# Weight sums by accumulating loads, and more blocks of seven products in the feed-forward part

## The chip, the cores and the metric

One NeuronCore of a Trainium2 chip runs the whole program. The time is device microseconds of that core. The kernel before takes 1552.08 us (median of three runs, 1551.42 to 1552.7).

## The reference

One layer of a conditioned hybrid decoder on 256 rows of width 2048, all in float32. The change concerns the second half:

```python
h2 = modulate(rms_norm(x, norm2_g[l]), sh2, sc2)
gate, up = jnp.split(h2 @ w_ffn_in[l], 2, axis=-1)          # 2048 -> 2 x 5632
x = x + g2 * ((jax.nn.silu(gate) * up) @ w_ffn_out[l])      # 5632 -> 2048
return rms_norm(x, final_g)
```

Ahead of it stand the modulation (a matrix-vector product with a 2048 x 12288 weight), one projection to 11264 columns, a gated linear recurrence, banded attention and three projections back.

## The kernel before, in words

**Three products for one.** Every float32 operand is split into a high part `hi` (rounded to float32r) and a low part `lo` = value - `hi`. `mm3` computes hi·hi, hi·lo and lo·hi: three matmuls for one product. Weights come in pieces of 128 x 1024 float32 (512 KB, an *item*): a load by SP's queue into one of five `raw` buffers, `hi` by a cast on ScalarE (ACT, four buffers), `lo` by a subtraction on VectorE (DVE, three buffers), and then the products on TensorE (PE).

**The planner.** `step(i)` writes out the order of everything around item i: the load of item i+5, `made` (an item that is computed, not loaded) of item i+4, `hi` of item i+3, `lo` of item i+2, the stages hung ahead of the item (`before`), and its products. Work between two slabs (`posts`) and side work (`sides`) goes in between, by a table of costs. Each engine runs its own instructions in this order. The only waits are for data and for a buffer to come free.

**Seven products rather than eight.** A pair of k tiles (2 x 128 rows of a weight) with two blocks of 512 columns and two blocks of 128 rows of activations is a 2 x 2 by 2 x 2 product of blocks. `seven()` computes it with seven block products by Winograd's scheme, with sums of weight blocks and of activation blocks formed ahead. It makes four items: a and b, the two loaded weight pieces (three of the four blocks are used as they are), x, a tile of two sums of weight blocks (`first`, L418 and L419), and y, a tile of two more sums that build on x (`second`, L424 and L425). All four sums are VectorE instructions of 128 x 512, into tiles called `made` in the slabs and a region of `last` in the sweeps. A plain pair is 24 matmuls of 128x512, a seven 21.

**The feed-forward part.** Slab 0 uses a plain form. Slabs 1 to 10 (`add_pair`) each compute 512 gate and 512 up columns with eight pairs of k tiles. The pairs k = 4, 8, 12 go by seven products (`SEVEN_1`). Then the second weight is swept: the first sweep (n = 0) does columns 0 to 1023 over all 44 k tiles, the second (n = 2) columns 1024 to 2047 over the first 36, and a tail does the rest. In each sweep the pairs k = 6, 10, ..., 34 go by seven (`SEVEN`), with one plain pair between two sevens. `parts_high` and `parts_low` split the sums of activations for a seven of a sweep (the tiles `ah` and `al`, L1370 on VectorE).

**Buffers.** `b4` is a pool of 25 general tiles of 4 KB per partition. The activations h and h2 and, at the end, `last` (the residual rows x2, the final gain fg and two sum tiles) lie in a pool of their own (`hp`), the modulation's weights, `made` and `ah` in two more (`araw`). `Halves.fetch` (L467) loads the modulation's weights on SP's queue; an instruction on VectorE (L496) uses one up and so hands the buffer back.

Of the kernel before, what the change touches and what calls it, by code (L numbers as in the profile page):

```python
# [74 lines left out]
def hybrid_layer(  # L75
# [8 lines left out]
    hp = ctx.enter_context(tc.tile_pool(name="hp", bufs=1))  # L84
    bp = ctx.enter_context(tc.tile_pool(name="bp", bufs=N_B4))
# [310 lines left out]

    SUMS = 4

    def seven(loads, where, act, bank, begin, end, made_in, post=None):

        got = {}

# [12 lines left out]
        def first(i):
            got.update({0: live[i - 2][0], 1: live[i - 1][0]})
            x = got["x"] = made_in(0)
            nc.vector.tensor_tensor(x[:, 0:512], block(0, 1), block(0, 0), op=ALU.subtract)  # L418
            nc.vector.tensor_tensor(x[:, 512:], block(0, 1), block(1, 1), op=ALU.subtract)  # L419
            return x  # L420

        def second(i):
            y, x = made_in(1), got["x"]
            nc.vector.tensor_tensor(y[:, 0:512], block(1, 1), x[:, 0:512], op=ALU.subtract)  # L424
            nc.vector.tensor_tensor(y[:, 512:], block(1, 0), y[:, 0:512], op=ALU.subtract)  # L425
# [1276 lines left out]
```

## Time and profile before

| | |
|---|---|
| median of three runs | 1552.08 us |
| the profiled execution | 1549.47 us, its span 1547.7 us, granted clock 0.997 |
| loads of the first feed-forward weight in a slab pair's form | 176 of 512 KB, median 4.2 us to landing |
| loads in the first sweep, second sweep | 44 and 36 of 512 KB, 4.3 and 3.4 us |
| HBM read | 394.72 MB, 258 GB/s with the writes over the span |
| POOL | 11 instructions, 3.7 us |

In the profile PE, DVE, ACT, POOL and SP are the five engines, PEld the weight load of TensorE, L12 a line of the kernel, and "raw", "hi", "lo" tiles by name without their numbers. The shortest way through it goes from the chain that ended last to the stage in which the change lies, and from there to the engine with least slack in that stage.

### The profile page before, as it was taken

To read this page: it belongs to the slowest core of one execution; us is meant where nothing else is said; L and a number is where in the kernel's file an instruction comes from. 1 tells how busy PE (TensorE), PEld (TensorE's weight loads), DVE (VectorE), ACT (ScalarE), POOL (GpSimd) and SP (SyncE) were. 2 spreads that over 40 slices of the span, in tenths; PEclk is the share of its full clock that TensorE was granted. 3 is DMA by queue.
4 is the path that set the end of the run, shared out by engine and by line. 5 is a ranking of instruction groups with operands and counts; after the bars stand their busy time and mean duration, and the time that the engine had idled before them with its cause. 6 is when DMAs were issued, how large, how long until landed. Compare 5 with 4: busy or idle time off the path is not lost.

```text
span 1547.7 us, 22116 instructions
## 1 busy us (share of the span) xinstructions
PE 1530.9 (99%) x8013; PEld 1314.2 (85%) x8013; DVE 1392.2 (90%) x1854; ACT 858.2 (55%) x1113; POOL 3.7 (0%) x11
## 2 busy tenths in 40 slices
PE   8999999999999999999999999999999999999997
PEld 7999999998878887888888788888888888888786
DVE  7889989889888887988988899999999999998998
ACT  4654443776855445444545655555555556664664
POOL 0000000000000000000000000000000000000000
PEclk9999999999999999999999999999999999999999
DMA  9999998666887797999999665565555666766563
GB/s 367 343 320 345 341 315 291 212 203 208 270 275 264 259 328 274 368 339 339 366 384 346 191 202 187 194 198 200 200 192 200 207 193 236 251 206 204 189 212 128
DMA packets 112909, 400.37 MB, mean 259 GB/s; under 512 B 12432, under 2 KB 12576, under 8 KB 112416
## 3 DMA queue, kind: packets, MB, share of 16 engines
q1 hardware_dynamic: 112192, 397.39, 74.5%
q8 instruction: 62, 1.02, 0.3%
q0 software_dynamic: 320, 1.06, 0.2%
q10 hardware_dynamic: 288, 0.52, 0.1%
q14 instruction: 47, 0.39, 0.1%
HBM read 394.72 MB, written 4.20 MB: 258 GB/s over the span
## 4 chain that ended last, share of the span: by engine, by line
PE 93%; DMA 4%; DVE 2%; issue 1%; ACT 0%; SPq 0%; DVEq 0%; ACTq 0%
PE pf L1352 9%; PE f L356 7%; PE f L357 7%; PE f L355 7%; PE wi L357 6%; PE wi L355 6%; PE wi L356 6%; PE wga L357 2%; PE wga L355 2%; PE wga L356 2%; PE wa L357 2%; PE wa L355 2%; PE wa L356 2%; PE wl L356 2%; PE wl L357 2%; PE wl L355 2%
## 5 line engine op out<-in xcount | busy, mean ns | idle before, releaser
L305 ACT CAST hi<-raw 128x1024 fp32r<-128x1024 f32 (+1 forms) x540 | 536.9, 1002 | 447.3 <-PE wi L356 77.2
L317 DVE TENSOR_TENSOR lo<-raw,hi 128x1024 fp32r<-128x1024 f32 (+1 forms) x540 | 618.7, 1159 | 66.0 <-issue 35.0
L357 PE MATMUL wi<-h_both,lo 128*128 128x256 f32 x800 | 227.3, 284 | 3.6 <-DVE lo L317 3.6
L355 PE MATMUL wi<-h_both,hi 128*128 128x256 f32 x800 | 228.0, 285 | 0.0
L356 PE MATMUL wi<-h_both,hi 128*128 128x256 f32 x800 | 227.0, 284 | 0.0
L355 PE MATMUL f<-hi,h_both 128*128 128x512 f32 x460 | 180.2, 392 | 0.0
L357 PE MATMUL f<-hi,h_both 128*128 128x512 f32 x460 | 179.0, 389 | 0.0
L356 PE MATMUL f<-lo,h_both 128*128 128x512 f32 x460 | 179.0, 389 | 0.0
L357 PEld LDWEIGHTS wi<-h_both,lo 128*128 128x128 f32 x800 | 154.2, 193 | 4.0 <-DVE lo L317 4.0
L356 PEld LDWEIGHTS wi<-h_both,hi 128*128 128x128 f32 x800 | 154.3, 193 | 0.2
L355 PEld LDWEIGHTS wi<-h_both,hi 128*128 128x128 f32 x800 | 154.3, 193 | 0.2
L305 ACT CAST hi<-made 128x1024 fp32r<-128x1024 f32 x60 | 63.4, 1057 | 112.8 <-PE f L357 111.3
L496 DVE CUSTOM_DVE_ANT_0 aw<-aw,crow,vec 128x1024 f32<-128x1024 f32 x79 | 100.6, 1278 | 6.2 <-DMA aw<-in_ada_t_dram 6.2
L496 DVE CUSTOM_DVE_ANT_0 aw<-aw,crow,modc 128x1024 f32<-128x1024 f32 x79 | 100.9, 1280 | 3.0 <-DMA aw<-in_ada_t_dram 2.8
L357 PEld LDWEIGHTS f<-hi,h_both 128*128 128x128 f32 x460 | 86.3, 188 | 18.0
L355 PEld LDWEIGHTS f<-hi,h_both 128*128 128x128 f32 x460 | 86.4, 188 | 17.8 <-issue 0.2
L356 PEld LDWEIGHTS f<-lo,h_both 128*128 128x128 f32 x460 | 86.4, 188 | 17.8 <-issue 0.2
L317 DVE TENSOR_TENSOR lo<-made,hi 128x1024 fp32r<-128x1024 f32 x60 | 73.4, 1225 | 25.9 <-PE f L356 20.7
L1352 PE MATMUL pf<-hi,fc 128*128 128x512 f32 x256 | 71.0, 389 | 0.0
L305 ACT CAST hi<-last 128x1024 fp32r<-128x1024 f32 x32 | 33.7, 1054 | 52.5 <-PE pf L1352 49.2
L1352 PEld LDWEIGHTS pf<-hi,fc 128*128 128x128 f32 x256 | 48.1, 188 | 10.0
L355 PE MATMUL wl<-hi,yh 128*128 128x512 f32 x128 | 52.5, 410 | 0.0
(355 smaller groups left out, 2940.4 us busy)
## 6 DMA issues: line engine op xcount, KB each, us to landing
raw<-in_w_f_dram SPq DMA_DIRECT2D x176, 512.0 KB, 4.2
raw<-in_w_in_dram SPq DMA_DIRECT2D x164, 512.0 KB, 7.1
aw<-in_ada_t_dram SPq DMA_DIRECT2D x158, 512.0 KB, 6.5
raw<-in_w_f2a_dram SPq DMA_DIRECT2D x44, 512.0 KB, 4.3
raw<-in_w_f2d_dram SPq DMA_DIRECT2D x36, 512.0 KB, 3.4
raw<-in_w_lru_dram SPq DMA_DIRECT2D x32, 512.0 KB, 6.5
raw<-in_w_att_dram SPq DMA_DIRECT2D x32, 512.0 KB, 7.8
raw<-in_w_o_dram SPq DMA_DIRECT2D x32, 512.0 KB, 8.3
```

The lines of the kernel that those rows point to most:

```text
L305: nc.scalar.copy(hi[:, cs], live[i][0][:, cs])
L317: nc.vector.tensor_tensor(lo[:, cs], raw[:, cs], f32(hi[:, cs]), op=ALU.subtract)
L355: nc.tensor.matmul(ps, lhsT=lh, rhs=rh, start=start, stop=False, skip_group_check=True)
L356: nc.tensor.matmul(ps, lhsT=lh, rhs=rl, start=False, stop=False, skip_group_check=True)
L357: nc.tensor.matmul(ps, lhsT=ll, rhs=rh, start=False, stop=stop, skip_group_check=True)
L496: nc.vector.tensor_tensor_reduce(out=r, in0=r, in1=crow[:, j * CH:(j + 1) * CH], op0=ALU.mult, op1=ALU.add, scale=1.0, scalar=dst if j els ...
L1352: nc.tensor.matmul(bank(t, n), lhsT=l[:, rows(t)], rhs=w[:, c0:c0 + 512], start=kt == 0 and k == 0, stop=kt == (EARLY - 2 if (t, n) == (1, ...
```

## The change

- **Sums of x by transfers.** `first` computes nothing any more. `fill` issues, on POOL's queue, two loads of 128 x 512 from the weight in HBM into a tile `wx` 16 steps ahead, and `add`, 11 steps ahead, two more such loads that add into it (`accum_op`). `second` still does two VectorE sums. Signs of the sums on the activations' side and of the combinations after it change to match.
- **Loads of used columns only.** The raw loads of a seven fetch 1.5 of 2 halves.
- **More sevens.** Slabs 1 to 8: k = 4, 6, 10, 12 (four of eight pairs), slab 9: 4, 6, 10, slab 10: 4, 6. In a slab the pairs run plain, plain, seven, seven, plain, seven, seven, plain. Sweeps: ten of 18 pairs, with turns `--77-77-77-77-77--` (7 a seven, - a plain pair) where it was plain, plain and then seven and plain in turn.
- **One pool.** h, h2, the modulation's weights, `ah`, `wx`, the y tiles, x2 and fg all come from `b4`, now 35 tiles. x2 and fg are fetched in halves, at chosen items.
- `f_parts` handles slabs with no, one or two pairs by seven.

```diff
-SEVEN = tuple(range(6, 36, 4))
-
-SEVEN_1, SLAB_7 = (4, 8, 12), 1
+N_SUM = (16, 11)
+SEVEN = (6, 10, 12, 14, 18, 22, 24, 26, 30, 34)
+
+SEVEN_1, SLAB_7, LAST_7 = (4, 6, 10, 12), 1, (3, 2)
+
+TURNS = "--77-77-77-77-77--"
...
-    hp = ctx.enter_context(tc.tile_pool(name="hp", bufs=1))
-    bp = ctx.enter_context(tc.tile_pool(name="bp", bufs=N_B4))
+    bp = ctx.enter_context(tc.tile_pool(name="bp", bufs=N_B4 + N_H + N_ADA))
...
+    def do_sum(j):
+        def do(i):
+            if items[i].sums is not None:
+                items[i].sums[j]()
+                load_time(CH)
+        return do
...
-        nc.sync.dma_start(raw[:, :cols], src)
-        live[i] = [raw, None, None, load_time(cols)]
+        cs = items[i].used
+        nc.sync.dma_start(raw[:, cs], src)
+        live[i] = [raw, None, None, load_time(cs.stop - cs.start)]
...
+        upto("fill", do_sum(0), i + N_SUM[0])
+        upto("add", do_sum(1), i + N_SUM[1])
...
+        def fill():
+            x = got["x"] = bp.tile([P, CH], F32, tag="b4", name="wx")
+            for j in range(2):
+                nc.gpsimd.dma_start(x[:, j * 512:(j + 1) * 512], block(0, 1))
+
+        def add():
+            for j in range(2):
+                nc.gpsimd.dma_start(got["x"][:, j * 512:(j + 1) * 512], block(j, j), accum_op=ALU.add)
 
         def first(i):
-            got.update({0: live[i - 2][0], 1: live[i - 1][0]})
-            x = got["x"] = made_in(0)
-            nc.vector.tensor_tensor(x[:, 0:512], block(0, 1), block(0, 0), op=ALU.subtract)
-            nc.vector.tensor_tensor(x[:, 512:], block(0, 1), block(1, 1), op=ALU.subtract)
-            return x
+            return got["x"], 0
 
         def second(i):
-            y, x = made_in(1), got["x"]
-            nc.vector.tensor_tensor(y[:, 0:512], block(1, 1), x[:, 0:512], op=ALU.subtract)
-            nc.vector.tensor_tensor(y[:, 512:], block(1, 0), y[:, 0:512], op=ALU.subtract)
-            return y
+            def raw(*kn):
+                l, c0 = where[kn]
+                return live[i - 3 + l][0][:, c0:c0 + 512]
+
+            y = bp.tile([P, CH], F32, tag="b4", name="wy")
+            nc.vector.tensor_tensor(y[:, 0:512], got["x"][:, 0:512], raw(1, 1), op=ALU.add)
+            nc.vector.tensor_tensor(y[:, 512:], y[:, 0:512], raw(1, 0), op=ALU.add)
+            return y, 1.3
...
         def parts_high():
-            hi = parts[0] = wp.tile([P, 8, P], F32R, tag="araw", name=f"ah{n}_{k}", bufs=N_ADA)
+            hi = parts[0] = b4(f"ah{n}_{k}", F32R, (8, P))
...
-                    t = wp.tile([P, CH], F32, tag="araw", name=f"aw{self.n}", bufs=N_ADA)
+                    t = bp.tile([P, CH], F32, tag="b4", name=f"aw{self.n}")
...
-        others = [k for k in range(0, EARLY, 2) if k not in SEVEN]
-        turns = others[:2] + [k for two in zip(SEVEN, others[2:]) for k in two]
+        start = len(items)
+        kinds = {"7": iter(SEVEN), "-": iter(k for k in range(0, EARLY, 2) if k not in SEVEN)}
+        turns = [next(kinds[c]) for c in TURNS]
```

How the change moves instructions, at three places. In the rows a number after a name tells tiles apart.

VectorE in the first sweep, before: the seven of k = 14 (items 528 to 531: a, b, x, y) behind the plain item 527. Two more plain items follow.

```order
L317 TENSOR_TENSOR lo527_12416<-raw527_12381,hi527_12404 128x1024
L418 TENSOR_TENSOR last_12197<-raw528_12390 128x512
L419 TENSOR_TENSOR last_12197<-raw528_12390,raw529_12402 128x512
L317 TENSOR_TENSOR lo528_12430<-raw528_12390,hi528_12414 128x512
L1370 TENSOR_TENSOR al0_14_12432<-fs3_9722,ah0_14_12418 128x896
L424 TENSOR_TENSOR last_12197<-raw529_12402,last_12197 128x512
L425 TENSOR_TENSOR last_12197<-raw529_12402,last_12197 128x512
L317 TENSOR_TENSOR lo529_12452<-raw529_12402,hi529_12428 128x1024
L317 TENSOR_TENSOR lo530_12470<-last_12197,hi530_12450 128x1024
L317 TENSOR_TENSOR lo531_12479<-last_12197,hi531_12468 128x1024
```

The same place in the changed order, the second seven of a double (k = 14, items 544 to 547) right behind the first (k = 12, items 540 to 543):

```order
L454 TENSOR_TENSOR wy_12607<-wy_12607,raw541_12558 128x512
L337 TENSOR_TENSOR lo541_12612<-raw541_12558,hi541_12587 128x1024
L337 TENSOR_TENSOR lo542_12630<-wx_12408,hi542_12610 128x1024
L337 TENSOR_TENSOR lo543_12637<-wy_12607,hi543_12628 128x1024
L337 TENSOR_TENSOR lo544_12652<-raw544_12605,hi544_12635 128x512
L1418 TENSOR_TENSOR al0_14_12656<-fs31_9812,ah0_14_12642 128x896
L453 TENSOR_TENSOR wy_12666<-wx_12494,raw545_12626 128x512
L454 TENSOR_TENSOR wy_12666<-wy_12666,raw545_12626 128x512
L337 TENSOR_TENSOR lo545_12671<-raw545_12626,hi545_12650 128x1024
L337 TENSOR_TENSOR lo546_12683<-wx_12494,hi546_12669 128x1024
L337 TENSOR_TENSOR lo547_12692<-wy_12666,hi547_12681 128x1024
```

The two sums of x are gone. `lo` of b, x and y of one seven is now followed by a, `al` and the sums of y of the next, where a plain pair's two `lo` stood.

VectorE in the second slab pair, before: the seven of k = 12 (items 324 to 327) behind two computed and two plain items.

```order
L317 TENSOR_TENSOR lo320_9030<-made_8976,hi320_9005 128x1024
L317 TENSOR_TENSOR lo321_9043<-made_9002,hi321_9028 128x1024
L317 TENSOR_TENSOR lo322_9052<-raw322_9000,hi322_9041 128x1024
L317 TENSOR_TENSOR lo323_9064<-raw323_9026,hi323_9050 128x1024
L418 TENSOR_TENSOR made_9073<-raw325_9048,raw324_9039 128x512
L419 TENSOR_TENSOR made_9073<-raw325_9048 128x512
L317 TENSOR_TENSOR lo324_9078<-raw324_9039,hi324_9062 128x1024
L424 TENSOR_TENSOR made_9094<-raw325_9048,made_9073 128x512
L425 TENSOR_TENSOR made_9094<-raw324_9039,made_9094 128x512
L317 TENSOR_TENSOR lo325_9099<-raw325_9048,hi325_9076 128x512
```

In the changed order, the end of the first seven of a double (k = 4, x and y are items 322 and 323) and the second (k = 6, items 324 to 327):

```order
L337 TENSOR_TENSOR lo322_9080<-wx_8845,hi322_9055 128x1024
L337 TENSOR_TENSOR lo323_9091<-wy_9052,hi323_9078 128x1024
L337 TENSOR_TENSOR lo324_9101<-raw324_9050,hi324_9089 128x1024
L453 TENSOR_TENSOR wy_9115<-wx_8894,raw325_9076 128x512
L454 TENSOR_TENSOR wy_9115<-wy_9115,raw324_9050 128x512
L337 TENSOR_TENSOR lo325_9120<-raw325_9076,hi325_9099 128x512
L337 TENSOR_TENSOR lo326_9133<-wx_8894,hi326_9118 128x1024
L337 TENSOR_TENSOR lo327_9145<-wy_9115,hi327_9131 128x1024
```

Here too the sums into the x tile are gone, and the second seven's sums of y and `lo` follow the first seven's without a plain pair between.

POOL in the slab pairs. Before, POOL has no instruction there. Now each double has four fills (L438) and behind them four adds (L442), x2 standing for two alike:

```order
L438 DMA wx_8845<-in_w_f1_dram 128x512 x2
L438 DMA wx_8894<-in_w_f1_dram 128x512 x2
L442 DMA wx_8845<-in_w_f1_dram 128x512 x2
L442 DMA wx_8894<-in_w_f1_dram 128x512 x2
L438 DMA wx_9002<-in_w_f1_dram 128x512 x2
L438 DMA wx_9093<-in_w_f1_dram 128x512 x2
L442 DMA wx_9002<-in_w_f1_dram 128x512 x2
L442 DMA wx_9093<-in_w_f1_dram 128x512 x2
L438 DMA wx_9227<-in_w_f1_dram 128x512 x2
```

A fill or an add of the next double stands behind the adds of this one on POOL.

More of the change, by code (lines that the diff above doesn't have):

```diff
@@ L276, in __init__ @@
             self.used, self.before = slice(*(used or (0, cols))), list(before)
+            self.sums = None
     items = []
     live = {}
-    at = {"load": 0, "made": 0, "hi": 0, "lo": 0}
+    at = {"fill": 0, "add": 0, "load": 0, "made": 0, "hi": 0, "lo": 0}
+    def do_sum(j):
[4 more added lines that the diff above has]
+        return do
     def do_load(i):
@@ L397, in hybrid_layer, with seven @@
     SUMS = 4
-    def seven(loads, where, act, bank, begin, end, made_in, post=None):
+    def seven(loads, block, by_k, act, bank, begin, end, post=None):
         got = {}
+        where = {(k, n): (k, n * 512) if by_k else (n, k * 512) for k in range(2) for n in range(2)}
         def products(*jobs):
@@ L430, in seven @@
             jobs = [(a, where[kn][1], to) for a, kn, to in plain if where[kn][0] == l]
-            cs = [c0 for _, c0, _ in jobs]
+            cs = [where[kn][1] for _, kn, _ in plain if where[kn][0] == l]
+            used = (min(cs), max(cs) + 512)
             items.append(Item(
-                loads[l], CH, products(*jobs), weight=0.25 * len(jobs), used=(min(cs), max(cs) + 512),
+                loads[l][:, slice(*used)], CH, products(*jobs), weight=0.25 * len(jobs), used=used,
             ))
         items.append(Item(first, CH, products((3, 0, "r"), (5, 512, "u")), weight=0.5))
+        items[-1].sums = fill, add
         items.append(Item(second, CH, products((4, 0, "q"), (2, 512, "10")), post, weight=0.5))
@@ L1192, in h2act @@
     def h2act(kt):
-        return h2["both"][:, kt, 0, :], h2["both"][:, kt, 1, :]
+        return h2["parts"][kt]
     def gate_f_post(s):
@@ L1215, in f_parts @@
     def f_parts(s, pts):
-        if 4 * s + 2 not in SEVEN:
+        seven_ = [j for j in range(2) if 4 * s + 2 * j in SEVEN]
+        if not seven_:
             fh, fl = b4(f"fh{s}", F32R), b4(f"fl{s}", F32R)
@@ L1288, in add_pair @@
         start = len(items)
-        for k in range(0, NK, 2):
+        sevens = SEVEN_1[:LAST_7[s - 9]] if s > 8 else SEVEN_1
+        others = [k for k in range(0, NK, 2) if k not in sevens]
+        for k in others[:2] + list(sevens[:2]) + others[2:3] + list(sevens[2:]) + others[3:]:
             loads = [w_f1[s + 11 * n][:, k * 512:(k + 2) * 512] for n in range(2)]
-            if k in SEVEN_1:
-                last = k == SEVEN_1[-1]
+            if k in sevens:
+                last = k == sevens[-1]
                 seven(
-                    loads, {(0, 0): (0, 0), (1, 0): (0, 512), (0, 1): (1, 0), (1, 1): (1, 512)}, act(k), bank,
-                    k == SEVEN_1[0], last,
-                    lambda i: wp.tile([P, CH], F32, tag="araw", name="made", bufs=N_ADA), shared if last else None,
+                    loads, lambda j, n, k=k: w_f1[s + 11 * n][:, (k + j) * 512:(k + j + 1) * 512], False, act(k), bank,
+                    k == sevens[0], last, shared if last else None,
                 )
@@ L1299, in add_pair @@
             for n in range(2):
-                items.append(Item(loads[n], CH, plain(k, n), gated_rows if (k, n) == (NK - 2, 1) else None))
+                items.append(Item(loads[n], CH, plain(k, n), gated_rows if (k, n) == (others[-1], 1) else None))
         if s == SLAB_7:
@@ L1466, in hybrid_layer @@
                 ))
+        end = len(items)
+        if n == 0:
+            items[end - 12].before.append(fetch(0, 0, 1))
+        else:
+            items[start + 8].before.append(fetch(0, "fg"))
+            items[end - 14].before.append(fetch(1, 0, 1))
+            items[end - 6].before.append(fetch(1, "fg"))
     for i, k in enumerate(range(EARLY, NH, 2)):
```

132 lines of the change are left out of this document (73 added, 59 removed).

## Prediction

> **What bounds the kernel now.** I read the page's totals and its chain of waits first, then the busy time by stretch, then single instructions of one period.
>
> ```profile
> span 1547.7 us, 22116 instructions
> PE 1530.9 (99%) x8013; PEld 1314.2 (85%) x8013; DVE 1392.2 (90%) x1854; ACT 858.2 (55%) x1113; POOL 3.7 (0%) x11
> PE 93%; DMA 4%; DVE 2%; issue 1%; ACT 0%; SPq 0%; DVEq 0%; ACTq 0%
> ```
>
> TensorE sets the time, and VectorE has a tenth of the span left. The windows view shows the stages: the nine slab pairs between two equal instructions (927.20 to 1309.20), the first and the second sweep, and three stretches ahead of them.
>
> ```profile
> core 0: us, PE busy (x) PEld busy (x) DVE busy (x) ACT busy (x) POOL busy (x), PEclk, DMA share, GB/s
> 927.20:1309.20 382.00, 382.00 (x1724) 317.10 (x1723) 354.43 (x432) 216.65 (x252) 0.00 (x0) 1.00 0.60 198
> 1309.20:1400.00 90.80, 90.80 (x406) 75.29 (x405) 88.49 (x100) 58.25 (x65) 0.00 (x0) 1.00 0.68 238
> 1400.00:1500.00 100.00, 99.54 (x437) 81.49 (x436) 92.66 (x106) 58.02 (x67) 0.00 (x0) 1.00 0.60 200
> 100.00:200.00 100.00, 100.00 (x798) 98.34 (x797) 93.06 (x132) 43.97 (x51) 0.00 (x0) 1.00 0.94 338
> 700.00:800.00 100.00, 100.00 (x455) 82.98 (x454) 89.32 (x94) 46.79 (x66) 1.70 (x3) 1.00 1.00 360
> ```
>
> In the stages that change, TensorE is never idle, at a granted clock of 1.00; VectorE is busy 93% in the slab pairs and 97% in the first sweep. The DMA engines move 198 to 238 GB/s there, and TensorE stood at full busy elsewhere with 338 and 360. So removed matmuls shorten the time as long as VectorE keeps up, and VectorE is nearly full.
>
> What a late VectorE does shows in the chain at the start of the second sweep, and in the rows of the two engines there:
>
> ```profile
> 1445.91 1.23 DVE lo L317
> 1449.97 5.44 PE pf L1352 x24
> 1460.70 5.44 PE pf L1352 x24
> 1470.99 5.44 PE pf L1352 x24
> 1481.19 5.44 PE pf L1352 x24
> ...
> 1446.58 0.39 PE L355 MATMUL pr<-hi,ah 128*128 128x512 f32 x1
> 1447.19 0.50 PE L356 MATMUL pr<-lo,ah 128*128 128x512 f32 x1 [0.22 <-DVE lo L317]
> ```
>
> One 128x512 matmul takes 5.44/24 = 0.2267 us. A period of one plain pair (24 matmuls) and one block of seven products (21) is 45 x 0.2267 = 10.20 us, which the last two starts show; the two before are 10.73 and 10.29, so 0.53 + 0.09 us were stalls. The first matmul of an item needs only `hi`, the second needs `lo`: it came 0.61 us after the first, 0.06 us after its `lo` ended (1445.91 + 1.22 = 1447.13).
>
> **The change part by part.** *Products.* Sevens go from 10 x 3 + 2 x 8 = 46 to 8 x 4 + 3 + 2 + 2 x 10 = 57. Each saves one product, three matmuls: 33 x 0.2267 = **-7.5 us** (21 matmuls in the slabs, 4.8 us; 12 in the sweeps, 2.7 us). That stands only if TensorE stays fed.
>
> *VectorE in the sweeps.* One period of before, from its timeline (start, duration):
>
> ```profile
> 1340.41 0.39 PE L355 MATMUL pp<-hi,ah 128*128 128x512 f32 x1
> 1340.66 1.05 ACT L305 CAST hi<-last 128x1024 fp32r<-128x1024 f32 x1 [1.66 <-PE pf L1352]
> 1341.74 1.22 DVE L317 TENSOR_TENSOR lo<-last,hi 128x1024 fp32r<-128x1024 f32 x1 [0.29 <-ACT hi L305]
> 1342.88 2.35 DVE L317 TENSOR_TENSOR lo<-raw,hi 128x1024 fp32r<-128x1024 f32 x2
> 1345.15 0.69 DVE L418 TENSOR_TENSOR last<-raw 128x512 f32<-128x512 f32 x1
> 1345.76 0.68 DVE L419 TENSOR_TENSOR last<-raw,raw 128x512 f32<-128x512 f32 x1
> 1346.36 0.69 DVE L317 TENSOR_TENSOR lo<-raw,hi 128x512 fp32r<-128x512 f32 x1
> 1346.96 1.08 DVE L1370 TENSOR_TENSOR al<-fs,ah 128x896 fp32r<-128x896 f32 x1
> 1347.96 0.69 DVE L424 TENSOR_TENSOR last<-raw,last 128x512 f32<-128x512 f32 x1
> 1348.68 0.69 DVE L425 TENSOR_TENSOR last<-raw,last 128x512 f32<-128x512 f32 x1
> 1349.29 1.22 DVE L317 TENSOR_TENSOR lo<-raw,hi 128x1024 fp32r<-128x1024 f32 x1
> 1350.43 1.22 DVE L317 TENSOR_TENSOR lo<-last,hi 128x1024 fp32r<-128x1024 f32 x1
> ```
>
> Successive starts cost 1.14 us for a `lo` of 1024 columns, 0.60 for one of 512 or a sum, 1.00 for `al`, 1.33 for the two sums of y. The change takes the two sums of x (L418, L419) off VectorE: a seven costs 0.60 + 3 x 1.14 + 1.33 + 1.00 = 6.35 us there and was 7.55. But the new turns put two sevens side by side with one plain pair: 2 x 6.35 + 2 x 1.14 = 14.98 us of VectorE against (21 + 21 + 24) x 0.2267 = 14.96 of TensorE. There is no slack left, so the order within the period decides.
>
> Call the four items of the first seven a, b, x, y and those of the second a', b', x', y'; let TensorE begin a at 0. ACT's `hi` of y begins at 0.25, when a buffer comes free (1340.66 against 1340.41), and `lo` of y begins at 1.33 (1341.74). VectorE then has, in the order it is given, `lo` a' (+1.14), `al'` (+0.60), the two sums of y' (+1.00), `lo` b' (+1.33), which ends 1.22 later: 1.33 + 1.14 + 0.60 + 1.00 + 1.33 + 1.22 = 6.62. TensorE has finished the first seven at 21 x 0.2267 = 4.76, a' at 5.44, and wants `lo` b' at 5.67. With the 0.06 us of above it waits 6.68 - 5.67 = **1.0 us**. What follows is in time: `lo` x' ends at 6.62 + 1.14 = 7.76, wanted at 6.68 + 5 x 0.2267 + 0.2267 = 8.04. Before, a plain pair stood in this place, 5.44 us of TensorE for 2.28 of VectorE. Ten double sevens in the two sweeps: **+10 us**. The lower bound is the engine's own excess with the 0.29 us that it idles for `hi` once a period, 14.98 + 0.29 - 14.96 = 0.3 us, or +3; I take the upper, since the order is fixed.
>
> The work in the sweeps that is not periodic (the sums after the first sweep, the product with the final gain, L1451) cost about 0.6 us at the start of the second sweep, by the periods above. With no slack, the gain's 128x1024 product among the sums of y' comes on top, at most another 1.22 us; I take **+0.9**.
>
> *VectorE in the slabs.* The same chain, without `al` and with whole columns the other way round:
>
> ```profile
> 1108.15 0.39 PE L355 MATMUL fp<-hi,h_both 128*128 128x512 f32 x1
> 1108.39 1.06 ACT L305 CAST hi<-made 128x1024 fp32r<-128x1024 f32 x1 [1.66 <-PE f L357]
> 1108.19 2.58 DVE L317 TENSOR_TENSOR lo<-made,hi 128x1024 fp32r<-128x1024 f32 x2 [0.30 <-PE f L356]
> 1110.84 2.36 DVE L317 TENSOR_TENSOR lo<-raw,hi 128x1024 fp32r<-128x1024 f32 x2
> ```
>
> `lo` a' begins 2.69 us after a's start (1110.84), the sums of y' 1.14 later, `lo` b' after 1.33 and `lo` x' 0.60 after that, ending 2.69 + 1.14 + 1.33 + 0.60 + 1.22 + 0.06 = 7.04. Here a has two products and b one, so TensorE wants the second matmul of x' at 30 x 0.2267 + 0.2267 = 7.03. It just fits: **0 us**, but 0.1 us more in each of the 18 double sevens would cost 2.
>
> *The transfers.* Fills and adds need no slot of the raw ring, and each add is issued 11 steps ahead. Per seven they bring 2 x 0.524 MB, and the raw loads lose 0.262, so a slab pair goes from 16 x 0.524 = 8.39 MB (in 42.4 us: 198 GB/s, as the window shows) to 8.39 + 4 x 0.786 = 11.53 MB in 41.8 us, 276 GB/s; the second sweep goes from 18.9 to 26.7 MB in 91 us, 293 GB/s. Both lie under 338. That holds if an accumulating byte costs a plain one. No row shows an accumulating transfer. The nearest software transfers are these:
>
> ```profile
> L1021 POOL DMA_DIRECT2D g<-g1d x2 | 1.1, 541 | 5.3 <-DMA g1d<-g_row 5.3
> ...
> g<-g1d POOLq DMA_DIRECT2D x2, 512.0 KB, 8.6
> ...
> raw<-in_w_f_dram SPq DMA_DIRECT2D x176, 512.0 KB, 4.2
> ```
>
> An issue takes POOL 0.54 us: four per seven are 2.2 us on an idle engine. New waits: an add waits on POOL for its fill, with only later fills behind it; ACT's `hi` of x waits for the add, with every later `hi` behind it, and so TensorE. From the add's place to that `hi` are seven steps of 41.8/24 = 1.74 us, 12.2 us, against 8.6 us to landing in the row. Below, an accumulate that costs nothing still moves nothing earlier: 0. Above, at three plain bytes each, the second sweep would be 26.7 + 2 x 5.24 = 37.2 MB, 103 us at 360 GB/s instead of 91, and the DMA engines would set the pace. I take **0**, near the plain rows, and keep the other end as a rival.
>
> The Trainium skill speaks against that: Collectives: The Full Stack, in the section on the bandwidth ceiling, says that a transfer that adds is slow not for the addition but for its two reads, which both go on the same ring. Two reads per added byte would make 31.9 MB in the second sweep, an estimate of 351 GB/s, just inside the 360 of the window above; by it the sum stays as it is, with nothing to spare. No run here shows it yet.
>
> *Waits that go.* The buffers of the modulation's weights become part of a larger pool, so SP no longer waits for VectorE to hand one back:
>
> ```profile
> SPq L467 <- DVE modc L496: 297.3, 98, 9.5
> ...
> 400.00:500.00 100.00, 99.07 (x444) 80.78 (x443) 87.72 (x125) 62.55 (x88) 0.00 (x0) 1.00 0.84 281
> 800.00:885.00 85.00, 84.10 (x387) 68.59 (x386) 73.95 (x98) 49.53 (x72) 0.00 (x0) 1.00 0.85 298
> ```
>
> Behind those waits on SP's queue stand raw loads. TensorE idles 0.93 and 0.90 us in the stretches where that could matter, so between 0 and -1.8: I take **-1.0**. The rest of the front keeps its order and its first 50 us are set by loads: 0. Fetching x2 and the gain in halves, and changed signs, cost no instruction: 0, behind TensorE's products.
>
> Sum: -7.5 + 10 + 0 + 0.9 + 0 - 1.0 = **+2.4 us**. The profiled execution took 1549.47 us (1.8 outside its span) and would become 1551.9; the median of the runs is 1552.08, 2.6 above it, and becomes **1554.5**. I tell apart 0.2% (3.1 us): below 1549.0 is faster, above 1555.2 slower. My forecast is no measurable change.
>
> **The rivals.** *The saving arrives whole.* If `lo` b' comes in time (the `al` of the second seven lands while VectorE waits for `hi` y, or instructions follow each other faster than the pitches above), the doubles cost 0 and the time is 1552.1 - 7.5 = 1544.6, or 1547.6 with the 0.3 us per double of the engine's excess. For it: periods of before keep 10.20 with VectorE at 97%. Against it: the 1447.19 row, where one late `lo` is paid at once.
>
> *The accumulating transfers fill the DMA engines* (slower). Place: sweeps first, then slab pairs. Raw loads then land late and every item waits. It decides where the bytes needed pass 338 to 360 GB/s: in the second sweep 30.8 to 32.8 MB, so from an accumulate of 1 + (30.8 - 26.7)/5.24 = 1.8 to 2.2 plain bytes; in a slab pair from 2.2 to 2.7. At three: two sweeps of +12 us, nine slab pairs of 15.7 MB, 43.7 us against 41.8, +17: 1552.1 - 8.5 + 41 = 1585. Against it: shares of 0.60 now. For it: 57 x 4 transfers of a kind that the trace lacks.
>
> *The change does not do what it says* (stays at 8 products somewhere): the new order has 33 matmuls fewer, so this has no chance of its own.
>
> **How the numbers follow.** Doubles stall, transfers are hidden: 0.45, 1551 to 1558, of which 0.25 lies within 0.2%, 0.19 above, 0.01 below. The saving arrives: 0.22, 1542 to 1549, all but 0.01 faster. DMA engines full: 0.25, 1555 to 1595, all but 0.01 slower. Something else: 0.08, 0.03 either way and 0.02 the same. Faster 0.25, same 0.29, slower 0.46. The range 1543.5 to 1580 holds the first, three quarters of the second and some three fifths of the third.
>
> **What would show it.** Right: the first sweep has five pauses of about 1 us, at the second matmul of b', put down to `lo`; periods of two sevens and a pair near 16.0 us, not 14.96; slab pairs 41.8 us; DMA share near 0.85 with landings of raw loads within 6 us. Wrong: no pause in the sweeps (the first rival), or pauses put down to raw loads or to `wx`, a DMA share near 1.0 and landings beyond 10 us (the second).

## The result and the profile after

The changed kernel takes 1561.82 us (median of six runs, 1558.66 to 1565.42) against 1551.49 beside it: ratio 1.0066, 95% interval 1.0051 to 1.0081. It is 10.3 us slower. The forecast was 1554.5, no measurable change: the range held the time, and the verdict did not hold, since 10.3 us is over three times the 3.1 us that the forecast tells apart.

The profiled execution took 1565.42 us, 3.6 above the median, so its stages hold some 3.6 us more than those of a usual execution. The page of the changed kernel:

```profile
span 1563.7 us, 22457 instructions
PE 1532.7 (98%) x7980; PEld 1307.1 (84%) x7980; DVE 1376.4 (88%) x1821; ACT 878.9 (56%) x1144; POOL 168.1 (11%) x239
q1 hardware_dynamic: 112624, 382.45, 69.5%
q0 software_dynamic: 25856, 60.84, 16.6%
```

VectorE has less to do, TensorE has 33 matmuls fewer, and the span is longer: waits were added. To find where, I cut both traces at the first matmul (hi·hi) of the same groups: the first projection (wi), the output projection (wo), slab 1 (f), and the tail (late). The slabs end at the last such matmul of f. The groups' rows before (count and shortest/median/longest ns, first and last start):

```profile
L355 PE MATMUL wi<-h_both,hi x800: 277/283/472, 33.5 to 355.6; 128*128 128x256 f32 x160
L355 PE MATMUL wo<-hi,mh x128: 389/389/476, 742.5 to 829.8; 128*128 128x512 f32 x128
L355 PE MATMUL f<-hi,h_both x460: 389/389/796, 884.1 to 1307.6; 128*128 128x512 f32 x154
L355 PE MATMUL late<-hi,fh x16: 278/283/283, 1533.4 to 1538.8; 128*128 128x256 f32 x16
```

and after:

```profile
L377 PE MATMUL wi<-h,hi x800: 277/283/468, 35.0 to 355.5; 128*128 128x256 f32 x160
L377 PE MATMUL wo<-hi,mh x128: 389/389/477, 740.6 to 827.8; 128*128 128x512 f32 x128
L377 PE MATMUL f<-hi,h x418: 389/389/793, 886.7 to 1309.8; 128*128 128x512 f32 x140
L377 PE MATMUL late<-hi,fh x16: 278/283/284, 1548.8 to 1554.2; 128*128 128x256 f32 x16
```

Differences of these starts, in us, for the profiled execution of each kernel of this study (the first columns are medians and the ratio to the kernel before beside it):

| kernel | median | ratio | to wi | wi to wo | wo to slab 1 | slabs | sweeps | tail |
|---|---|---|---|---|---|---|---|---|
| before | 1551.49 | | 33.5 | 709.0 | 141.6 | 423.5 | 225.8 | 14.3 |
| after | 1561.82 | 1.0066 | 35.0 | 705.6 | 146.1 | 423.1 | 239.0 | 14.9 |
| e1_al_early | 1554.61 | 1.0008 | 33.2 | 705.9 | 144.3 | 422.8 | 230.8 | 15.0 |
| e2_plain_loads | 1558.38 | 1.0037 | 33.1 | 707.5 | 141.9 | 423.0 | 236.9 | 14.9 |
| e3_x2_early | 1557.67 | 1.0033 | 34.6 | 705.5 | 143.8 | 423.0 | 234.1 | 15.0 |
| e4_single_turns | 1547.87 | 0.9968 | 33.4 | 704.7 | 145.0 | 422.9 | 224.6 | 14.9 |
| e5_slab1_late | 1561.12 | 1.0063 | 33.5 | 704.9 | 145.1 | 422.7 | 239.1 | 14.6 |
| e6_before_counts | 1545.24 | 0.9960 | 33.6 | 705.0 | 141.6 | 423.5 | 224.6 | 15.3 |
| e7_dve_sums | 1590.61 | 1.0255 | 33.7 | 705.5 | 140.6 | 442.0 | 252.1 | 14.9 |
| c2_slab_singles | 1552.07 | 1.0006 | 33.8 | 704.8 | 141.5 | 430.5 | 224.6 | 14.8 |
| e8_own_pool | 1551.26 | 1.0003 | 34.9 | 709.6 | 147.7 | 424.1 | 224.6 | 14.6 |
| d3_deeper | 1623.00 | 1.0457 | 33.1 | 775.0 | 154.0 | 419.8 | 224.7 | 14.6 |
| d4_ten_spread | 1622.50 | 1.0458 | 33.8 | 772.0 | 154.1 | 420.6 | 221.9 | 16.7 |
| d5_deeper_late | 1540.86 | 0.9933 | 33.5 | 704.9 | 140.7 | 419.5 | 224.7 | 14.6 |

Between the two profiles 3.4 us are gained from wi to wo, 0.4 in the slabs (where 4.8 were to come), 4.5 lost ahead of slab 1 and 13.2 in the sweeps, with 1.5 ahead of wi and 0.6 in the tail. Of the 3.4, 1.6 lie in wi itself, which starts 1.5 us later and ends as before (last start 355.6 and 355.5); the other 1.8 lie between that and wo (386.9 and 385.1). The chain of waits of the changed kernel shows the sweeps' loss, one entry (`lo`) per double seven in the first sweep:

```profile
1333.11 5.44 PE pf L1400 x24
1343.80 1.23 DVE lo L337
1349.22 5.44 PE pf L1400 x24
...
1397.32 9.21 DMA x<-x1d
```

A period of two sevens and a plain pair takes 1349.22 - 1333.11 = 16.11 us, where its matmuls need 14.96. The double that begins at 1338.39 in the timeline of both engines:

```profile
1338.39 0.39 PE L377 MATMUL pp<-hi,ah 128*128 128x512 f32 x1
1338.19 1.23 DVE L337 TENSOR_TENSOR lo<-wx,hi 128x1024 fp32r<-128x1024 f32 x1 [0.67 <-issue]
1339.72 1.23 DVE L337 TENSOR_TENSOR lo<-wy,hi 128x1024 fp32r<-128x1024 f32 x1 [0.30 <-ACT hi L325]
1340.86 0.68 DVE L337 TENSOR_TENSOR lo<-raw,hi 128x512 fp32r<-128x512 f32 x1
1341.46 1.08 DVE L1418 TENSOR_TENSOR al<-fs,ah 128x896 fp32r<-128x896 f32 x1
1342.47 0.68 DVE L453 TENSOR_TENSOR wy<-wx,raw 128x512 f32<-128x512 f32 x1
1343.18 0.69 DVE L454 TENSOR_TENSOR wy<-wy,raw 128x512 f32<-128x512 f32 x1
1343.80 1.22 DVE L337 TENSOR_TENSOR lo<-raw,hi 128x1024 fp32r<-128x1024 f32 x1
...
1343.83 0.39 PE L377 MATMUL pf<-hi,ah 128*128 128x512 f32 x1
1345.07 0.50 PE L378 MATMUL pf<-lo,ah 128*128 128x512 f32 x1 [0.85 <-DVE lo L337]
1345.40 0.39 PE L379 MATMUL pf<-hi,al 128*128 128x512 f32 x1
```

Here `pp` is a's product, and the rows from 1340.86 on are `lo` a', `al'`, the two sums of y' and `lo` b'. `lo` b' ends 1345.02 - 1338.39 = 6.63 us after a's start. The second matmul of b' starts 1.24 us after the first, not 0.23, and the third 0.33 after that: 1.01 + 0.11 us lost.

### The profile page after: what moved, and what is told of

It reads as the page before. It is cut to its first block, busy times and chain, and to the rows that moved or that the text cites. A ratio compares the mean times of both kernels' runs of the same rounds, so it can differ in the third digit from the quotient of the medians.

```text
span 1563.7 us, 22457 instructions
## 1 busy us (share of the span) xinstructions
PE 1532.7 (98%) x7980; PEld 1307.1 (84%) x7980; DVE 1376.4 (88%) x1821; ACT 878.9 (56%) x1144; POOL 168.1 (11%) x239
## 3 DMA queue, kind: packets, MB, share of 16 engines
q1 hardware_dynamic: 112624, 382.45, 69.5%
q0 software_dynamic: 25856, 60.84, 16.6%
## 4 chain that ended last, share of the span: by engine, by line
PE 91%; DMA 4%; DVE 3%; issue 1%; ACT 0%; SPq 0%; POOL 0%; DVEq 0%; ACTq 0%
PE pf L1400 8%; PE f L377 7%; PE f L379 7%; PE wi L379 7%; PE f L378 7%; PE wi L378 7%; PE wi L377 7%; PE wl L379 2%; PE wl L377 2%; PE wga L379 2%; PE wga L377 2%; PE wl L378 2%; PE wgl L377 2%; PE wgl L379 2%; PE wga L378 2%; PE wa L379 2%
## 5 line engine op out<-in xcount | busy, mean ns | idle before, releaser
L379 PE MATMUL wi<-h,lo 128*128 128x256 f32 x800 | 227.3, 284 | 2.2 <-DVE lo L337 2.2
L377 PE MATMUL wi<-h,hi 128*128 128x256 f32 x800 | 228.1, 285 | 0.0
L378 PE MATMUL wi<-h,hi 128*128 128x256 f32 x800 | 227.3, 284 | 0.0
L377 PE MATMUL f<-hi,h 128*128 128x512 f32 x418 | 164.0, 392 | 0.0
L379 PE MATMUL f<-hi,h 128*128 128x512 f32 x418 | 162.8, 390 | 0.0
L378 PE MATMUL f<-lo,h 128*128 128x512 f32 x418 | 162.8, 389 | 0.0
L379 PEld LDWEIGHTS wi<-h,lo 128*128 128x128 f32 x800 | 154.4, 193 | 2.4 <-DVE lo L337 2.4
L377 PEld LDWEIGHTS wi<-h,hi 128*128 128x128 f32 x800 | 154.4, 193 | 0.2
L378 PEld LDWEIGHTS wi<-h,hi 128*128 128x128 f32 x800 | 154.3, 193 | 0.2
L379 PEld LDWEIGHTS f<-hi,h 128*128 128x128 f32 x418 | 78.5, 188 | 16.3
L378 PEld LDWEIGHTS f<-lo,h 128*128 128x128 f32 x418 | 78.5, 188 | 16.2 <-issue 0.2
L377 PEld LDWEIGHTS f<-hi,h 128*128 128x128 f32 x418 | 78.5, 188 | 16.2 <-ACT pa L726 0.2
L337 DVE TENSOR_TENSOR lo<-wx,hi 128x1024 fp32r<-128x1024 f32 x57 | 69.7, 1222 | 24.1 <-issue 21.0
L438 POOL DMA_DIRECT2D wx<-in_w_f_dram x74 | 41.0, 575 | 368.3 <-DVE lo L337 186.9
L337 DVE TENSOR_TENSOR lo<-wy,hi 128x1024 fp32r<-128x1024 f32 x57 | 69.7, 1222 | 5.4 <-ACT hi L325 2.7
L442 POOL DMA_DIRECT2D wx<-in_w_f_dram x74 | 66.5, 994 | 45.0 <-DMA wx<-in_w_f_dram 41.9
```

The lines of the kernel that those rows point to most:

```text
L337: nc.vector.tensor_tensor(lo[:, cs], raw[:, cs], f32(hi[:, cs]), op=ALU.subtract)
L377: nc.tensor.matmul(ps, lhsT=lh, rhs=rh, start=start, stop=False, skip_group_check=True)
L378: nc.tensor.matmul(ps, lhsT=lh, rhs=rl, start=False, stop=False, skip_group_check=True)
L379: nc.tensor.matmul(ps, lhsT=ll, rhs=rh, start=False, stop=stop, skip_group_check=True)
L438: nc.gpsimd.dma_start(x[:, j * 512:(j + 1) * 512], block(0, 1))
L442: nc.gpsimd.dma_start(got["x"][:, j * 512:(j + 1) * 512], block(j, j), accum_op=ALU.add)
```

## The experiments

Two theories. **Order**: the order of VectorE's work in double sevens makes `lo` late. **Transfers**: the accumulating loads slow the other loads. Each experiment is read by the stage of the table that moves.

**1. `al` of a second seven earlier.** The activation split is hung three items further ahead when the item before is a computed one, so that it fills the 0.67 us of the row at 1338.19.

```diff
-        items[-3].before.append(parts_high)
-        items[-2].before.append(parts_low)
+        early = 3 * (len(items) >= 4 and items[-2].sums is not None)
+        items[-3 - early].before.append(parts_high)
+        items[-2 - early].before.append(parts_low)
```

> Of a double seven's second block, the split of the activation sums (ah on ACT, al on VectorE) is issued three items earlier, so that al stands ahead of lo of x of the first seven, where VectorE idled 0.67 us. Theory order (VectorE's order of work makes lo b' late): lo b' then ends 1338.19 + 0.3 + 1.14 + 1.14 + 0.60 + 1.33 + 1.22 = 1344.0 where it ended at 1345.0, and TensorE wants it at 1344.06: the ten pauses of 1.1 us fall to 0 to 0.3 us each, 8 to 11 us off, 1551 to 1554. Theory transfers (the accumulating loads slow the raw loads): nothing about the transfers changes, so 1560 to 1563.

Measured 1554.61 (1552.71 to 1556.5), 7.2 less, just short of the 8 to 11 expected; the sweeps fall from 239.0 to 230.8. The waits of TensorE in the sweeps in the changed kernel, and then the row for `lo` b' here, two waits for ten; the other two rows stay at 2.9 and 0.4 us:

```profile
PE pf L378 <- DVE lo L337: 8.5, 10, 0.9
PE pf L1400 <- DVE lo L337: 2.9, 1, 2.9
PE pq L378 <- DVE lo L337: 0.4, 1, 0.4
```

```profile
PE pf L378 <- DVE lo L337: 0.9, 2, 0.5
```

Order holds for the pauses: nothing about the transfers was touched. A double for which no wait is listed still loses a little: a period runs from 1328.69 to 1343.80, 15.11 us, 0.15 over its matmuls. The account of the slabs' doubles below says why.

**2. Plain loads in place of adding ones.**

```diff
-                nc.gpsimd.dma_start(got["x"][:, j * 512:(j + 1) * 512], block(j, j), accum_op=ALU.add)
+                nc.gpsimd.dma_start(got["x"][:, j * 512:(j + 1) * 512], block(j, j))
```

> The adding loads become plain loads into the same tile (so the tile x holds one block and no sum, which is left out of the computation); their number, size and place stay. Theory transfers: if an adding load costs the DMA engines about twice a plain one, the DMA share falls from about 0.9 to 0.8 in the sweeps, the late raw loads at 817 and 847 us and the late x2 rows shrink, and 3 to 6 us go. Theory order: the pauses at b' stay at 1.1 us, and no more than the 7 us outside the doubles can go: 1555 to 1562, with the ten pauses unchanged.

Measured 1558.38, 3.4 less. The doubles keep their pauses (sweeps 236.9), and the stretch ahead of slab 1 falls from 146.1 to 141.9: that loss is the adds'. In that stretch of the changed kernel ACT, and behind it VectorE and TensorE, waits for raw loads, as here:

```profile
863.16 1.04 ACT L325 CAST hi<-raw 128x1024 fp32r<-128x1024 f32 x1 [4.16 <-DMA raw<-in_w_f_dram]
```

The experiment also prices the adding load. The windows of the stretch ahead of slab 1 and of the slabs in the changed kernel, then the slabs' window and the software queue here (a window's last two numbers are DMA share, the time that packets took by 16 engines, and GB/s):

```profile
800.00:890.00 90.00, 86.25 (x388) 68.48 (x387) 72.86 (x98) 49.42 (x73) 22.54 (x32) 1.00 1.04 349
890.00:1310.00 420.00, 419.05 (x1876) 343.68 (x1875) 375.86 (x454) 250.17 (x295) 95.72 (x133) 1.00 0.87 259
```

```profile
890.00:1310.00 420.00, 419.05 (x1872) 343.77 (x1871) 376.56 (x453) 250.61 (x297) 71.08 (x134) 1.00 0.75 259
q0 software_dynamic: 18560, 60.84, 11.2%
```

Over the whole span the software queue held the DMA engines 16.6% of 1563.7 = 259.6 us and here 11.2% of 1557.3 = 174.4, with 60.84 MB in both. Adds are 57 x 2 x 0.262 = 29.9 MB; as plain loads they take 174.4 x 29.9/60.84 = 85.7, as adds 85.2 more: 2.0 plain loads. The adds also go in packets of 2 KB and the plain loads in packets of 4 KB, but that is not the reason: in the changed kernel's trace a packet of an add took 176 ns in the median, a plain 2 KB packet of the hardware queue 84 and a plain 4 KB packet 159. Collectives: The Full Stack in the Trainium skill (the section on the bandwidth ceiling) says that the adding step of a collective is slow because it needs two source reads; the trace agrees with a price of two and does not show the reads. With it the DMA engines stood at 0.85 to 0.87 in slabs and sweeps, not full, but at 1.04 from 800 to 890 us (0.83 in the kernel before).

**3. x2 fetched earlier.** `fetch(0, 0, 1)` at 18 instead of 12 items ahead of the sweep's end.

> The first halves of the rows x2, which are fetched 12 items ahead of the end of the first sweep and land 9.2 us later, are fetched 18 items ahead. Both theories: VectorE no longer waits 6.96 us for them at the start of the second sweep, behind which lo and so TensorE were 3.0 us late and some 1.5 us more; 3 to 4.5 us less in executions in which they were late, 1557 to 1560 in the median. If the fetch takes another raw load's place in the same crowd, nothing is gained: 1561.

Measured 1557.67, 4.2 less (sweeps 239.0 to 234.1). In the changed kernel VectorE waits for x2 in front of the work that TensorE needs next:

```profile
DVE x L1446 <- DMA x<-x1d: 7.0, 1, 7.0
```

Here that wait is gone, and TensorE's wait of 2.9 us (the row with L1400 above) with it.

**4. Sweeps with eight single sevens.**

```diff
-SEVEN = (6, 10, 12, 14, 18, 22, 24, 26, 30, 34)
+SEVEN = tuple(range(6, 36, 4))
-TURNS = "--77-77-77-77-77--"
+TURNS = "--7-7-7-7-7-7-7-7-"
```

> The sweeps go back to the turns of the kernel before: eight sevens, each behind a plain pair, with the sums of x still by accumulating loads. Theory order: the ten pauses go (-11.2) and four products of three matmuls come back in two sweeps (+4 x 3 x 0.2267 = 2.7): 8.5 less, 1553. Theory transfers: 4 x 0.786 MB fewer of 53 MB in the sweeps change little: -1 to +2, 1561 to 1564.

Measured 1547.87, 14.0 less than the changed kernel where 8.5 were expected, and 0.9968 (0.9954 to 0.9982) of the kernel before. The sweeps take 224.6 us, 14.4 less: the ten pauses (11.2), the non-periodic ones, the wait for x2 (in time here without an earlier fetch), less 2.7 for the products. TensorE has no wait left in them. In the sweeps, then, ten sevens with fewer products were slower than eight.

**5. Slab 1's sevens late.**

```diff
-        sevens = SEVEN_1[:LAST_7[s - 9]] if s > 8 else SEVEN_1
+        sevens = SEVEN_1[:LAST_7[s - 9]] if s > 8 else SEVEN_1[2:] if s == SLAB_7 else SEVEN_1
...
+        for k in others[:5] + list(sevens) + others[5:] if s == SLAB_7 else others[:2] + list(sevens[:2]) + others[2:3] + list(sevens[2:]) + others[3:]:
```

> Slab 1 computes only k = 10 and 12 by sevens, behind five plain pairs, so its first adding loads start some 27 us later, out of the stretch from 800 to 887 us in which the DMA engines stood at 1.04 of their share. Theory transfers (there they make raw loads late): the stretch from the first product of the output projection to slab 1, 146.1 us in the changed kernel, 143.8 to 144.3 in two variants, 141.6 before and 141.9 with plain loads, falls to 142; the pause of 0.94 us in slab 1 behind a late sum of activations goes too; two products come back (+1.4). Together 2 to 4 us less than the changed kernel, 1558 to 1560. Rival (the pooled buffers, not the transfers, delay that stretch): it stays at 144 to 146 and the time at 1562 to 1563.

Measured 1561.12: a miss. The stretch stays at 145.1. That is the number of the rival, but the pooled buffers are there in experiments 2 and 7 too, where the stretch takes 141.9 and 140.6, so the rival falls. POOL's timeline shows what the edit did not move; the changed kernel's first fill and an add, then this kernel's first fill:

```profile
823.52 1.07 POOL L438 DMA_DIRECT2D wx<-in_w_f_dram  x2 [98.22 <-PE wo L379]
...
848.53 0.91 POOL L442 DMA_DIRECT2D wx<-in_w_f_dram  x1 [9.01 <-DMA wx<-in_w_f_dram]
```

```profile
822.57 1.07 POOL L438 DMA_DIRECT2D wx<-in_w_f_dram  x2 [99.16 <-DVE pa L718]
```

A fill waits for nothing but a free tile (an add also for its fill to land, 9.01 us in the row above), so the first fill leaves at 823 us wherever its seven stands. "16 steps ahead" sets the order on POOL and no time.

**6. The products of before, with the sums by transfers.** `SEVEN_1 = (4, 8, 12)` in every slab pair, pairs in the order of k, sweeps as in 4.

> The products of the kernel before (k = 4, 8, 12 in every slab pair, eight per sweep, each behind a plain pair), with the sums of x by transfers and all the rest of the change: the transfers' own effect. Theory order: no seven follows another, so nothing is late in slabs or sweeps; the slabs take 423.5 us and the sweeps 225 as before. What is left is the stretch ahead of slab 1 (+2 to +4) and the tail (+0.6), less the stall at 400 to 500 us that went (-0.9): 1552 to 1555. Theory transfers: taking two VectorE sums from each seven is itself worth time: 1548 to 1550.

Measured 1545.24, 0.9960 (0.9948 to 0.9972) of the kernel before: faster than both theories expected. Variant 4, which has seven sevens more in the slabs, is not faster (0.9968; the intervals overlap). The stretch ahead of slab 1 is 141.6 as before, so at these counts the transfers cost nothing there. The gain lies from wi to wo (4.0, of which 1.8 behind the last product of wi) and in the sweeps (1.2).

**7. x sums on VectorE.** The changed kernel with `first` as two VectorE sums, whole raw loads, no fills and adds.

> The changed kernel with the x sums put back on VectorE (two 128x512 sums per seven, whole raw loads, no software transfers). Theory order: a period of two sevens and a plain pair takes VectorE 14.98 + 4 x 0.60 = 17.4 us against 14.96 of TensorE, so the ten doubles of the sweeps cost about 2.4 to 3.5 us each and every slab pair, whose VectorE work of 41.0 us on 41.8 grows by 3 x 1.2 = 3.6 over the kernel before, some 2 to 4: 1580 to 1600. Rival (VectorE's volume does not matter, the transfers did the harm): 1552 or less.

Measured 1590.61. Slabs 442.0, sweeps 252.1. In the slabs' window VectorE is at 404.97 of 420 us:

```profile
890.00:1310.00 420.00, 410.69 (x1788) 325.19 (x1787) 404.97 (x512) 240.84 (x286) 0.00 (x0) 1.00 0.57 191
```

So in the changed arrangement the transfers save 29 us, and most of the loss is the arrangement's. The part ahead of slab 1 is the transfers': here, without any, that stretch takes 140.6.

**8. Single sevens in slabs.** Pairs of a slab as plain, seven, plain, seven, plain, seven, seven, plain; slab 1 as in 5; sweeps as in 4.

> Sweeps with eight single sevens, slab 1 with two late sevens, and in the other slabs plain pairs and sevens in turn as far as they go (plain, seven, plain, seven, plain, seven, seven, plain): seven double sevens of slabs rather than eighteen. Theory order: against the variant with single turns alone (1547.9) the stretch ahead of slab 1 gives 2.5, the late sum of activations 1.3, eleven doubles of 0.17 us 1.9, and two products cost 1.4: 1543 to 1545. Rival (a seven early in a slab is late for another reason, the work between slabs): 1547 to 1550.

Measured 1552.07: a miss, the slabs at 430.5. A seven in second place needs a PSUM bank (a place where TensorE's products add up) that the work between slabs still reads; TensorE's waits there:

```profile
PE fu L377 <- DVE fc L1262: 5.6, 8, 1.1
```

With two plain pairs first and one last, four sevens have one plain pair left to part them: doubles are the price of a fourth seven. The stretch ahead of slab 1 is 141.5 here and 145.1 in 5, with the same slab 1. The next slab differs: it starts with single sevens, and POOL issues two fills and two adds at a time rather than four and four. That the bursts make the raw loads late is an inference from this pair and from 6. Fewer transfers ahead of slab 1 are a rival: POOL issues 26 there in this kernel, 22 in 6, 28 in 5 and 30 in the changed kernel. Neither was tried alone.

**9. The modulation's weights in two buffers of their own again,** on variant 6.

```diff
-                    t = bp.tile([P, CH], F32, tag="b4", name=f"aw{self.n}")
+                    t = wp.tile([P, CH], F32, tag="araw", name=f"aw{self.n}", bufs=N_ADA)
```

> The variant with the products of the kernel before and the sums by transfers (1545.24), with one thing undone: the modulation's weights again have two buffers of their own rather than tiles of the large pool. Theory pool (SP's wait for those two buffers held raw loads back): the stretch from the first product of the projection to the first of the output projection, 709.0 us before and 705.0 in that variant, goes back to 708 to 709, and the time to 1548 to 1549. Rival (the 4 us come from somewhere else in the change, such as smaller loads or the executions' own spread): 1545 as it was.

Measured 1551.26 (1549.7 to 1557.28), 6.0 more where 3 to 4 were expected, the whole gain of variant 6: 1.0003 (0.9992 to 1.0014) of the kernel before. From wi to wo it takes 709.6 us, behind the last product of wi 387.4 (385.1 in 6), and SP's waits are back:

```profile
SPq L498 <- DVE modc L527: 296.0, 98, 9.5
```

The profiled execution was the slowest of its runs; why it took 147.7 us ahead of slab 1 is not known.

**10 and 11. One more `hi` and one more `lo` buffer, splits one item earlier.** Both with three sevens in slab 1 (plain, plain, 7, -, 7, -, 7, -), doubles in slabs 2 to 8 and single sevens in 9 and 10; 10 with eight single sevens per sweep, 11 with ten, three of them doubled, and with the edits of experiments 1 and 3.

> Eight single sevens per sweep, three single sevens in slab 1, and from slab 2 on two doubles in a slab as in the changed kernel, with one more hi and one more lo buffer (the large pool is 2 tiles smaller) and hi and lo split one item earlier. Theory order: with lo of y no longer waiting for a buffer the doubles of slabs lose their 0.17 us each, so the slabs take 424.0 - 6 x 0.68 = 419.9 us rather than 423.4; the stretch ahead of slab 1 takes 141.6: together about 4 less than with the products of before, 1541. Rival (earlier hi meets raw loads that have not landed, at 259 GB/s): slabs at 423 or more, 1545 or more.

> The same with ten sevens per sweep, spread so that three in each sweep follow another directly rather than five (turns plain, plain, 7, -, 7, -, 77, -, 7, -, 77, -, 7, -, 77), al of a second seven ahead as in the first experiment and x2 fetched earlier. Theory order: four sevens more save 2.7 us and the six doubles cost 0 to 0.5 each: 1539 to 1542, sweeps at 222 to 224. Rival (VectorE has no room for ten sevens wherever they stand, since it holds 14.98 us against 14.96 per double): sweeps at 226 or more, 1544 or more.

Measured 1623.0 and 1622.5: misses. By stage both numbers of theory order came: slabs 419.8 and 420.6 (419.9 expected), sweeps 221.9 with ten sevens (222 to 224), with a tail of 16.7 that gives 2 of that back. But from wi to wo 66 and 63 us were lost, and 12 more ahead of slab 1, where the large pool had two tiles fewer and every split stood earlier. The main waits of 10 there, and a window of it (TensorE's granted clock is the third number from the end):

```profile
PE wi L377 <- ACT h L586: 28.1, 8, 5.4
PE wl L377 <- ACT yh L839: 15.8, 1, 15.8
500.00:600.00 100.00, 84.13 (x365) 68.03 (x363) 75.02 (x112) 45.96 (x63) 0.00 (x0) 0.91 0.75 256
```

The waits are not the whole loss: TensorE was also busy 24.9 us longer than in variant 12 with the same 7995 matmuls (1547.9 against 1523.0), at a granted clock of 0.979 against 0.999. Which of the two, the pool or the earlier splits, did that was not tried.

**12. The same, from slab 1 on only.** Every fifth `hi` and every fourth `lo` is a tile of the large pool; eight single sevens per sweep.

```diff
+        more = int(i >= deep[0])
-        upto("hi", do_hi, i + N_HI)
-        upto("lo", do_lo, i + N_LO)
+        upto("hi", do_hi, i + N_HI + more)
+        upto("lo", do_lo, i + N_LO + more)
```

> The same products as in the variant with one more hi and lo buffer and eight single sevens, but the extra buffers are single tiles of the large pool and are used, with the splits one item earlier, from slab 1 on only; ahead of it everything is as in the changed kernel. Theory order: ahead of slab 1 705 and 141.6 us as with the products of before, slabs 420.3, sweeps 224.2, the rest 14.8: a span of 33.6 + 705 + 141.6 + 420.3 + 224.2 + 14.8 = 1539.5 (the milestones before it included), 1541 by the runs: faster than every other kernel here. Rival (the tiles taken from the large pool or the slab's doubled transfers crowd the stretch ahead): 143 to 146 us there and 1544 or more.

Measured 1540.86 (1539.67 to 1543.08), as expected, 0.9933 (0.9919 to 0.9947) of the kernel before: faster than both kernels and every variant. TensorE does not idle in the slabs and sweeps, and the second matmul of x' comes in time:

```profile
931.00:1300.00 369.00, 369.00 (x1661) 305.90 (x1660) 331.00 (x393) 219.16 (x258) 91.61 (x126) 1.00 0.89 268
1310.00:1400.00 90.00, 90.00 (x399) 74.53 (x398) 79.80 (x85) 55.32 (x59) 20.37 (x28) 1.00 0.87 273
...
1065.64 0.39 PE L382 MATMUL fr<-hi,hs 128*128 128x512 f32 x1
1065.87 0.39 PE L383 MATMUL fr<-lo,hs 128*128 128x512 f32 x1
1066.10 0.39 PE L384 MATMUL fr<-hi,hs 128*128 128x512 f32 x1
```

## Why the prediction was right or wrong

The time lay in the range, which says little: it was 36.5 us wide and held most of three cases. The verdict failed, and the time lay 3.8 us above the 1551 to 1558 of the forecast's own case. The mechanism of that case, the pauses of the doubles in the sweeps, was right. Three terms at or near nothing were mis-sized (the doubles of the slabs, the transfers, the waits that go), and two waits were not in the sum (x2, and sums of activations in slab 1). Term by term, from the profiled pair:

- **Products, -7.5:** right. Variant 12's slabs are 4.0 us shorter with six sevens more than before (36 for 30), 6 x 0.68 = 4.1 expected.
- **Doubles of the sweeps, +10:** right in place and instruction, 1.2 short in size. `lo` b' was put at 6.62 us and ended at 6.63; a pause costs 1.12, with the late start of the matmul behind it, so 11.2. Experiments 1 and 4 show the cause.
- **Doubles of the slabs, 0:** the step said that `lo` x' just fits (7.04 against 7.03) and that 0.1 us more would cost 2. The chain came out as written, and the price of it was wrong. The rows of such an x' in the changed kernel are

```profile
1074.22 1.22 DVE L337 TENSOR_TENSOR lo<-wx,hi 128x1024 fp32r<-128x1024 f32 x1
1075.26 0.39 PE L377 MATMUL fr<-hi,hs 128*128 128x512 f32 x1
1075.50 0.50 PE L378 MATMUL fr<-lo,hs 128*128 128x512 f32 x1
1075.84 0.40 PE L379 MATMUL fr<-hi,hs 128*128 128x512 f32 x1
```

  where `lo` x' ends at 1075.44 and the second matmul starts 0.24 us after the first instead of 0.23, 0.01 late as forecast. But the third starts 0.34 after the second, 0.11 late, as it does behind the pauses of the sweeps (0.33 there), and the ones that follow are late by some 0.05 more: 0.17 on average by the starts of the 17 outside slab 1, so 3.1 us for all 18. So a chain with no slack was priced at nothing, because only the late matmul itself was counted. In slab 1 four sums of activations (`hs`, missing from the forecast's sum) stand on VectorE in front of `lo` a' from 901.47 to 902.40 us and cost another 1.3. Together they eat 4.4 of the slabs' 4.8.
- **Non-periodic work, +0.9:** one pause of 0.66 (at `pq`). But "fetching x2 in halves: 0" failed: a load that the kernel before issued at the sweep's start (1309.3 us) is issued at 1397.32 and lands 7.0 us after VectorE wants it, and the profile has about 4.5 us of it. Experiment 3 shows it. The step asked what instructions the edit adds and not how late the moved load lands.
- **Transfers, 0:** an adding byte costs 2.0 plain ones, between the bounds of one and three, and within the 1.8 to 2.2 from which the rival was to decide in the second sweep; but the DMA engines are not full in slabs and sweeps, as chosen, and the rival's mechanism did not decide there (raw loads landed in 6.4 us in the slabs, 6.8 and 5.0 in the sweeps by median, a little beyond the 6 that was named at most). It did so in a place that the step had not looked at: the stretch ahead of slab 1, where the share rose from 0.83 to 1.04, +4.5 in the profile, +2.2 to 3.5 in experiments 1, 3, 4 and 5, +0.3 with plain loads, -1.0 with no transfers (7). A high share alone does not do it: experiments 6 and 8 have 1.01 and 1.03 there and lose nothing. The fills of slab 1 were costed in the stage that uses them, and POOL issues the first of them 63 us ahead of that stage.
- **Waits that go, -1.0 (0 to -1.8):** -3.4 in the profile from wi to wo, but 1.6 of it only makes up for the later start of wi. Behind the last product of wi it is -1.8, and steadily so: 386.9 us before, 385.1 or 385.2 in the changed kernel and in experiments 1 to 8 and 12, 387.4 in 9. That is the far end of the bound, though the view's idle time there is 0.93: by the starts its two pauses cost 1.5, for the reason given at the slabs. The wait that mattered was also not only that of raw loads. In that stretch VectorE itself waited for the modulation's weights in the kernel before, which it does not in the changed kernel and does again in 9:

```profile
DVE aw L496 <- DMA aw<-in_ada_t_dram: 8.7, 10, 1.6
```

  Experiment 9 shows the pool as the cause. It loses 6.0 by medians; 2.3 of that is this stretch, and where the rest lies in a usual execution is not known.

In the sum: -7.5 + 11.2 + 3.1 + 1.3 + 0.7 + 4.5 + 4.5 - 3.4, with 0.6 in the tail, less 1.0 for two pauses of before in the second sweep that are gone and 1.5 more ahead of wi, is 15.5, against 15.95 between the profiled executions and 10.3 between the medians. The two profiled executions lie 3.6 above and 2.0 below their medians, so a usual pair has some 5.6 us less of these; in which terms is not known.

The first rival (the saving arrives whole) fell by the pauses; what it named, `al` while VectorE waits, is experiment 1. The second named the right resource and the wrong place.

## What to carry to other kernels

Before removing work from the engine that sets the end, write out the in-order work of the engine that feeds it over one period: here the sum (14.98 against 14.96 us) said that it was full, and the chain said which instruction would be late, to 0.01 us. A chain that "just fits", repeated 18 times, is a cost, since here 0.01 us of lateness cost 0.17; one more `hi` and one more `lo` buffer and one step of lookahead (with 14 doubles for 18) turned it into a gain of 4.0 in the slabs. Price a pause by the starts of the matmuls around it, not by the idle time that a view lists: 0.85 us of idle cost 1.12. Fills that wait for nothing but free buffers run as far ahead as these let them, so they are to be costed where they will be issued.

## What the runs showed of the hardware

An adding transfer from HBM cost the DMA engines 2.0 times a plain one, and POOL 0.99 us per issue instead of 0.58 for a fill. Software transfers with tile rows of 2 KB, which the trace of experiment 2 has as packets of 4 KB, moved 60.84 MB in 174.4 us of all engines (349 GB/s), as fast as the hardware queue's 382.45 MB in 69.7% of 1557.3 us (352 GB/s). A matmul that had to wait for its operand made the one behind it start 0.11 us late as well, whether it had waited 1.01 us (1345.07) or 0.01 (1075.50). Where TensorE was idle for 16 of 100 us, its granted clock was 0.91 in that window (experiment 10).
